# All tiles of a diffusion-transformer block on multiples of 64 bytes, the large ones on multiples of 2048

## The chip, the cores and the metric

The kernel runs on one core of a Trainium2 chip. The metric is the device time of one execution in microseconds; three executions were timed, and a further one was recorded by the hardware profiler. Everything about the profile comes from that one.

A core has a matrix engine (TensorE, PE in the profile, with its weight loads as PEld), VectorE (DVE), ScalarE (ACT), GpSimd (POOL), a queue engine (SP) and 16 DMA engines. Operands lie in an on-chip memory of 128 partitions. A tile has the same byte address in each of its partitions, and that address is what this change is about.

## What is computed

One layer of a diffusion backbone over 256 latent tokens and 256 context tokens of width 2048, in fp32:

```python
mod = jax.nn.silu(c) @ w_mod[layer] + b_mod[layer]
h = modulate(rmsnorm(x, norm_g[layer, 0]), sh_a, sc_a)
hc = modulate(rmsnorm(ctx, norm_g[layer, 0]), csh_a, csc_a)
# one input projection, split: latent attention q/k/v, the recurrent branch, the gates
attn_l = block_attention(q_l, concat(k_c, k_l), concat(v_c, v_l))
hgo_c, s_f, s_b = hgrn2_bidirectional(*hg_c[:6], zero_state, zero_state)
hgo_l, _, _ = hgrn2_bidirectional(*hg_l[:6], s_f, s_b)
out_l = merge_branches(attn_l, hgo_l, hg_l[6], gl_l, ...)     # two branch products, gates, w_out
x = x + gt_a * rmsnorm(out_l, norm_g[layer, 1])
h = modulate(rmsnorm(x, norm_g[layer, 2]), sh_f, sc_f)
x = x + gt_f * rmsnorm(swiglu(h, w_ffn_in[layer], w_ffn_out[layer]), norm_g[layer, 3])
```

The feed-forward width is 44 × 128 = 5632. The weights are read from the chip's main memory once; the profile counts 375 MB of reads.

## The kernel before

**How a product is made.** To keep fp32 accuracy, each operand is split into a high part H and a rest L, and a product is three matmuls: weight H by activation H, weight H by activation L, weight L by activation H. A weight block arrives by DMA as a tile `raw` (128 × 2048, 1 MB, three buffers); `split_w` makes `wH` with a ScalarE copy (L100) and `wL` with a VectorE subtraction (L102), in halves of 1024 columns, three buffers each. Activations are kept split. Tile `hx` (128 × 2 × 16 × 2 × 256: stream, block of the width, H or L, token) holds both streams' activations, and later, unit by unit, the merged branches, the feed-forward input and the feed-forward middle. Eight more units of 512 columns lie in the buffers `hC`. `cqkv` holds the split latents of the attention.

**The forms of a matmul.** One operand is stationary (loaded as weights, 128 columns), the other moves through (256 or 512 columns).

- `mm3` (L136): weights stationary, three matmuls. In `project` with two streams the moving operand is 512 wide, half of it from each stream; with one stream it is 256 wide. The first six blocks go into the sums `pre` while their activations are still being made.
- `mm_wide` (L140, L141): the two products with weight H are one matmul, since H and L of an activation lie side by side in `hx`: 512 columns; then weight L by activation H, 256 columns. The gate blocks (`ps`) and the feed-forward input (`psf`) use it.
- `project_tok` (L816): the activation is stationary and the weights move, 512 wide, into sums `pst` of 128 tokens by 512 channels. The output projection and the feed-forward output use it. A unit of the activation serves as six matmuls: two halves of the tokens, three products. In the last column block of some passes the weights are split into other tiles (`split_into`): into unused units of `hx`, or into `hC` buffers named `wl`.
- L754: the two branch products, 256 wide, moving `hx` (attention) and then `hC` (recurrent branch).

**Order.** The stages follow one another: modulation and first blocks (to about 150 us), the recurrent heads (to 566), gates and attention (to 822), branch products (to 915), output projection (to 1005), norm (to 1044), then feed-forward input and output in three parts each. A scheduler puts the instructions of each engine into one order ahead of time; it works with the sizes of the operations.

**Where the tiles lie.** Pools are laid out one after another in the order of their opening: `cp` (constants and `hx`), `wp` (`raw`, `wH`, `wL`), `ap` (`hC`), `bp` (four-unit tiles and `cqkv`), `wk` (small and middle-sized work tiles). Inside a pool the tiles lie in order of first use, each rounded up to 32 bytes. `cp` starts at byte 16,512, a multiple of 64. Its first tiles are `ones` (512 bytes), `epst` (4, rounded to 32), `sm` (924, to 928), `c0` (520, to 544), `cn` (3584), `cst` (8192), `A1` and `SH1` (128 each). Three of these are an odd number of 32-byte steps, so `hx` comes to byte 30,560, which is 32 past a multiple of 64 and 1888 past a multiple of 2048; `cn`, `cst` and `kr` are 32 past a multiple of 64 too. `wp` starts at 99,072, and from there `raw`, `wH`, `wL`, `hC` and the `bp` tiles all lie 768 past a multiple of 2048, that is, on multiples of 256. The later half of `wk` (from the tile `rdec` on) is again 32 past a multiple of 64.

Of the constants, `ones` is written once by VectorE at L62 and read by the sums of squares (`norm_x` at L212, `latent` at L383, L553); `cn` is loaded by one DMA from ScalarE's queue (L367) and read first by `rope` (L395). `rstd_tok` and `rstd_bcast` are called by nothing.

Of the kernel before, what the change touches and what calls it, by code (L numbers as in the profile page):

```python
# [7 lines left out]
F32 = mybir.dt.float32  # L8
F32R = mybir.dt.float32r
U32 = mybir.dt.uint32  # L10
AF = mybir.ActivationFunctionType
ALU = mybir.AluOpType
PSUM = bass.MemoryType.PSUM

P = 128
T = 256
D = 2048
KD = D // P
NH = 8
# [7 lines left out]
def block_kernel(  # L27
# [21 lines left out]
    nc = tc.nc  # L49

    cp = ctx.enter_context(tc.tile_pool(name="cp", bufs=1))
# [3 lines left out]
    wk = ctx.enter_context(tc.tile_pool(name="wk", bufs=1))  # L55
    pj = ctx.enter_context(tc.tile_pool(name="pj", bufs=4, space=PSUM))
    px = ctx.enter_context(tc.tile_pool(name="px", bufs=4, space=PSUM))
    dp = ctx.enter_context(tc.tile_pool(name="dp", bufs=1, space=bass.MemoryType.DRAM))


    ones = cp.tile([P, P], F32, name="ones")
    nc.vector.memset(ones, 1.0)  # L62
    epst = cp.tile([P, 1], F32, name="epst")
    nc.vector.memset(epst, EPS)

    sm = cp.tile([P, 231], F32, name="sm")
    nc.sync.dma_start(sm, small)
# [6 lines left out]
    ogt = sm[:, 230:231]  # L74
    c0 = cp.tile([P, 130], F32, name="c0")
    nc.scalar.dma_start(c0, consts[:, 0:130])
    ident = c0[:, 0:128]
    sel = c0[:, 128:130]
    cn = cp.tile([P, 896], F32, name="cn")
    perm = cn[:, 0:128]  # L80
# [67 lines left out]

    def rstd_tok(sums, n, tag):

        pt = px.tile([P, 512], F32, tag="px", name="ptok")
        for hf in range(2):
            for i, a in enumerate(sums):
                nc.tensor.matmul(pt[:, hf:hf + 1], a[:, hf * P:(hf + 1) * P], ones[:, 0:1],
                                 start=(hf == 0 and i == 0), stop=(hf == 1 and i == len(sums) - 1))
        return rstd_bcast(pt, n, tag)

    def rstd_bcast(pt, n, tag):
        rt = wk.tile([P, 2], F32, tag="rtok", name="rtok")
        nc.scalar.activation(rt, pt[:, 0:2], AF.Sqrt, bias=epst, scale=1.0 / n)  # L160
        nc.vector.reciprocal(rt, rt)
        dg = wk.tile([P, 2, P], F32, tag="dg", name="dg")
        pb = px.tile([P, 512], F32, tag="px", name="pbc")
        for hf in range(2):
            nc.vector.tensor_scalar(dg[:, hf], ident, rt[:, hf:hf + 1], None, op0=ALU.mult)
            nc.tensor.matmul(pb[:, hf * P:(hf + 1) * P], ones, dg[:, hf], start=(hf == 0), stop=(hf == 1))
        r = wk.tile([P, T], F32, tag=tag, name="rb")
        nc.scalar.copy(r, pb[:, 0:T])
        return r


# [3 lines left out]

    cst = cp.tile([P, D], F32, tag="cst", name="cst")[:, 0:KD * 32].rearrange("p (k m) -> p k m", m=32)
    nc.gpsimd.memset(cst, 0.0)
    nc.vector.tensor_copy(cst[:, :, 0:2], cv)

    A1 = cp.tile([P, KD, 2], F32, name="A1")  # L180
    SH1 = cp.tile([P, KD, 2], F32, name="SH1")

    hx = cp.tile([P, 2, KD, 2, T], F32R, name="hx")

# [91 lines left out]
    for g, nk in enumerate(GROUPS + [0, 0]):  # L278
# [3 lines left out]
        for kt in range(nt):  # L282
            if nk:
                raw = ahead.pop(0) if ahead else load_w(wm1[tile_no])
                tile_no += 1
                n = 256 * nk
                per = 2048 // n
                for kk in range(per):
                    k = kt * per + kk
                    nc.tensor.matmul(pm[32 * (k % 4):32 * (k % 4) + 32, 0:n], cst[:, k], raw[:, kk * n:(kk + 1) * n],  # L290
                                     start=(k < 4), stop=(k >= KD - 4))
# [9 lines left out]
        pt = px.tile([P, 512], F32, tag="px", name="pt")  # L301
# [20 lines left out]
    nc.vector.reciprocal(lbm, lbm)  # L322
    lb = cp.tile([P, 2, NH], F32, name="lb")
    oml = cp.tile([P, 2, NH], F32, name="oml")
    nc.vector.tensor_tensor(lb, lbt[:, 0], lbm, op=ALU.mult)
    nc.vector.tensor_scalar(oml, lb, -1.0, 1.0, op0=ALU.mult, op1=ALU.add)


    mod2 = cp.tile([P, 4, KD], F32, name="mod2")
    cbt = []  # L330
# [35 lines left out]

    nc.scalar.dma_start(cn, consts[:, 130:1026])  # L367

# [20 lines left out]

    kr = cp.tile([P, 2 * T], F32, name="kr")  # L390
    latent([0, 1], (0, 1), 512, kvgt, ckvs, 256, ("f", "kk"))
# [52 lines left out]
    def hgrn_head(h):  # L444
# [11 lines left out]
        def gate_chain(d, psf):  # L456
# [12 lines left out]
            qsv = qs.rearrange("p (n t) -> p n t", n=4)  # L469
            dec = wk.tile([P, 5], F32, tag=f"dec{d}", name=f"dec{d}")  # L470
            rdec = wk.tile([P, 4], F32, tag="rdec", name="rdec")
            fc = f[:, T:2 * T]
# [207 lines left out]
    def att_s(i, A):  # L680
# [4 lines left out]
        for qb in range(2):  # L685
# [5 lines left out]
            for n, (a, b) in enumerate(((0, 0), (0, 1), (1, 0))):  # L691
                nc.tensor.matmul(psS, qr[a][rr, qsl], krs[b][rr, :], start=False, stop=(n == 2))  # L692
            mx = wk.tile([P, 4], F32, tag="mx", name="mx", bufs=2)
            nc.vector.reduce_max(mx[:, 0:1], psS, axis=mybir.AxisListType.X)  # L694
# [73 lines left out]
    b2 = bm.rearrange("p (a k) -> p a k", k=KD)  # L768
    gts = cp.tile([P, 2, KD], F32, name="gts")
    A2 = cp.tile([P, KD], F32, name="A2")  # L770
    SH2 = cp.tile([P, KD], F32, name="SH2")
    nc.vector.tensor_tensor(SH2, mod2[:, 1], b2[:, 3], op=ALU.add)
# [46 lines left out]
    def sqrt_table(dep):  # L819

        t_ = wk.tile([P, 1], F32, tag="rdec", name="tbl")
        nc.scalar.activation(t_, dep, AF.Sqrt)

    def rstd_part(i, hf):

        rt = cp.tile([P, 1], F32, name=f"rt{i}{hf}")
        nc.vector.tensor_reduce(rt, ssq[:, i, hf], axis=mybir.AxisListType.X, op=ALU.add)
        nc.scalar.activation(rt, rt, AF.Sqrt, bias=epst, scale=1.0 / D)
        nc.vector.reciprocal(rt, rt)
        return rt  # L830
# [9 lines left out]
    r1 = []  # L840
    ssq = cp.tile([P, 3, 2, 4], F32, name="ssq")
    for c in range(4):
# [279 lines left out]
```

## Time and profile before

| | us |
|---|---|
| median of 3 timed runs (lowest, highest) | 1770.2 (1769.6, 1770.48) |
| the profiled execution | 1770.05 |
| its span, first to last instruction | 1768.3 |
| mean granted TensorE clock | 0.992 |

The profile gives, for each engine, its busy time and what ended its idle time; it groups instructions by source line, engine, operation and tiles. In `psf<-hx,wH 128*128 128x512` the sum `psf` is made from `hx` and `wH`, with a stationary operand of 128 × 128 and a moving one of 128 × 512. [...] The clock column is the share of the full TensorE clock that was granted.

### The profile page before, as it was taken

How to read it: one execution, taken by the hardware profiler on the slowest of the kernel's cores; microseconds unless marked ns; L12 is line 12 of the kernel's file. 1: busy time of each engine (PE TensorE's matmuls, PEld its weight loads, DVE VectorE, ACT ScalarE, POOL GpSimd, SP SyncE). 2: the span in 40 equal slices, each digit the busy share in tenths (PEclk: the TensorE clock that was granted, in tenths of full speed). 3: DMA queues.
4: the chain of work that ended last, by engine and by line, in shares of the span. 5: the costliest groups of instructions: out<-in, count | busy, mean ns of one | idle time of the engine just before them, and what ended most of it. 6: DMA issues, size and time to landing. Idle time of an engine off the chain costs nothing.

```text
span 1768.3 us, 24307 instructions
## 1 busy us (share of the span) xinstructions
PE 1719.5 (97%) x9696; PEld 1455.7 (82%) x9696; DVE 1114.2 (63%) x1702; ACT 781.7 (44%) x1162; POOL 55.6 (3%) x85
## 2 busy tenths in 40 slices
PE   5898999999999999999999899999999999999997
PEld 3457988888889888889998698888888888888886
DVE  5335777776768766666764687776445555555555
ACT  5224433333334544445544654444444444344443
POOL 1100000000000000001210000000000000000000
PEclk9999999999999999999999899999999999999999
DMA  9884355554556565578765457776555555555553
GB/s 385 324 331 164 122 194 209 191 197 168 194 180 227 208 226 215 191 262 316 277 233 184 163 208 271 289 283 259 190 190 191 189 184 187 191 186 187 188 189 119
DMA packets 59329, 382.87 MB, mean 217 GB/s; under 512 B 7024, under 2 KB 7568, under 8 KB 15952
## 3 DMA queue, kind: packets, MB, share of 16 engines
q1 hardware_dynamic: 54000, 365.85, 57.3%
q0 software_dynamic: 4352, 13.90, 2.1%
q8 instruction: 76, 1.25, 0.3%
q10 hardware_dynamic: 864, 1.57, 0.2%
q14 instruction: 37, 0.30, 0.0%
HBM read 374.99 MB, written 6.31 MB: 216 GB/s over the span
## 4 chain that ended last, share of the span: by engine, by line
PE 96%; DMA 2%; DVE 1%; ACT 1%; issue 0%; DVEq 0%; SPq 0%; ACTq 0%
PE ps L136 20%; PE pst L816 19%; PE psf L140 18%; PE psf L141 9%; PE ps L140 7%; PE psb L754 5%; PE pre L136 4%; PE ps L141 3%; PE psf L915 1%; PE pm L290 1%; DMA raw<-in_wm_dram 1%; PE psS L692 1%; PE po L716 1%; PE psS L689 1%; PE pv L664 1%; PE pq L648 1%
## 5 line engine op out<-in xcount | busy, mean ns | idle before, releaser
L102 DVE TENSOR_TENSOR wL<-raw,wH 128x1024 fp32r<-128x1024 f32 x480 | 588.2, 1227 | 458.4 <-ACT wH L100 456.6
L100 ACT CAST wH<-raw 128x1024 fp32r<-128x1024 f32 x480 | 501.6, 1046 | 745.2 <-PE ps L136 194.7
L140 PE MATMUL psf<-hx,wH 128*128 128x512 f32 x1344 | 470.8, 393 | 0.0
L141 PE MATMUL psf<-hx,wL 128*128 128x256 f32 x1344 | 374.9, 279 | 0.0
L136 PE MATMUL ps<-hx,wH 128*128 128x512 f32 (+1 forms) x1312 | 334.1, 343 | 1.3 <-ACT lat L380 1.3
L140 PEld LDWEIGHTS psf<-hx,wH 128*128 128x128 f32 x1344 | 251.8, 187 | 60.0
L141 PEld LDWEIGHTS psf<-hx,wL 128*128 128x128 f32 x1344 | 251.8, 187 | 0.3
L136 PEld LDWEIGHTS ps<-hx,wH 128*128 128x128 f32 x1312 | 225.0, 188 | 31.3 <-ACT lat L380 1.5
L816 PE MATMUL pst<-wH,hx 128*128 128x512 f32 x800 | 237.2, 396 | 0.0
L136 PE MATMUL ps<-hx,wL 128*128 128x512 f32 (+1 forms) x656 | 225.1, 343 | 1.2 <-DVE wL L102 1.2
L140 PE MATMUL ps<-hx,wH 128*128 128x512 f32 x512 | 184.4, 399 | 0.0
L816 PEld LDWEIGHTS pst<-wH,hx 128*128 128x128 f32 x800 | 150.5, 188 | 36.5
L349 DVE CUSTOM_DVE_ANT_0 raw<-raw,cb 128x2048 f32<-128x2048 f32 x64 | 146.2, 2284 | 42.6 <-DMA raw<-in_wm_dram 41.9
L141 PE MATMUL ps<-hx,wL 128*128 128x256 f32 x512 | 143.7, 281 | 0.0
L816 PE MATMUL pst<-wL,hx 128*128 128x512 f32 x400 | 143.5, 396 | 0.0
L136 PEld LDWEIGHTS ps<-hx,wL 128*128 128x128 f32 x656 | 123.7, 189 | 16.6 <-DVE wL L102 1.4
L140 PEld LDWEIGHTS ps<-hx,wH 128*128 128x128 f32 x512 | 96.0, 188 | 23.2 <-issue 1.7
L141 PEld LDWEIGHTS ps<-hx,wL 128*128 128x128 f32 x512 | 96.2, 188 | 2.4 <-DVE mx L694 1.1
L816 PEld LDWEIGHTS pst<-wL,hx 128*128 128x128 f32 x400 | 75.3, 188 | 18.4
L136 PE MATMUL pre<-hx,wH 128*128 128x512 f32 x192 | 66.0, 424 | 4.6 <-ACT hx L220 4.5
L136 PEld LDWEIGHTS pre<-hx,wH 128*128 128x128 f32 x192 | 37.5, 201 | 26.0 <-ACT hx L220 10.9
L754 PE MATMUL psb<-hx,wH 128*128 128x256 f32 x256 | 46.8, 282 | 0.0
(427 smaller groups left out, 1742.0 us busy)
## 6 DMA issues: line engine op xcount, KB each, us to landing
raw<-in_wm_dram SPq DMA_DIRECT2D x96, 1024.0 KB, 5.2
raw<-in_wfi_dram SPq DMA_DIRECT2D x84, 1024.0 KB, 4.8
raw<-in_win_dram SPq DMA_DIRECT2D x73, 1024.0 KB, 4.8
raw<-in_wfo_dram SPq DMA_DIRECT2D x44, 1024.0 KB, 4.8
raw<-in_wbr_dram SPq DMA_DIRECT2D x16, 1024.0 KB, 5.9
raw<-in_wout_dram SPq DMA_DIRECT2D x16, 1024.0 KB, 4.8
raw<-in_wqk_dram SPq DMA_DIRECT2D x4, 1024.0 KB, 5.3
sgd<-sgx POOLq DMA_DIRECT2D x16, 256.0 KB, 5.5
```

Source lines behind the costliest of these rows:

```text
L100: nc.scalar.copy(H, raw[:, o:o + n])
L102: nc.vector.tensor_tensor(L, raw[:, o:o + n], H.bitcast(F32), op=ALU.subtract)
L136: nc.tensor.matmul(o, l, r, start=(first and i == 0), stop=(last and i == len(seq) - 1))
L140: nc.tensor.matmul(ps, w[0], act.rearrange("p e t -> p (e t)"), start=first, stop=False)
L141: nc.tensor.matmul(ps[:, 0:T], w[1], act[:, 0, :], start=False, stop=last)
L290: nc.tensor.matmul(pm[32 * (k % 4):32 * (k % 4) + 32, 0:n], cst[:, k], raw[:, kk * n:(kk + 1) * n], start=(k < 4), stop=(k >= KD - 4))
L349: nc.vector.tensor_tensor_reduce(out=raw, in0=raw, in1=cbt[0], scale=1.0, scalar=0.0, op0=ALU.mult, op1=ALU.add, accum_out=mod2[:, i // KD ...
L648: nc.tensor.matmul(pq[:, i * T:(i + 1) * T], l, r, start=(k == 0 and i == 0 and z == 0), stop=(k == 3 and i == 1 and z == 2))
L664: nc.tensor.matmul(pv[:, i, :], ckvs[:, k, l, ts_], r, start=(i == 0 and k == 0 and z == 0), stop=(i == 1 and k == 1 and z == 2))
L689: nc.tensor.matmul(psS, qn[a][:, i * T + qb * P:i * T + (qb + 1) * P], kn[b], start=(n == 0), stop=False)
L754: nc.tensor.matmul(ps[:, br * T:(br + 1) * T], l, r, start=(br == 0 and k == 0 and z == 0), stop=(br == 1 and k == NH - 1 and z == 2))
L816: mm = nc.tensor.matmul(ps[hf], l, r, start=(k == 0 and n == 0), stop=(k == nk - 1 and n == 2))
```

## The change

Sizes of tiles are padded, some tiles change their pool or their place in it, and slices keep the part that is used. No instruction of the computation is added or taken away. The diff, cut to its core:

```diff
-    ones = cp.tile([P, P], F32, name="ones")
-    nc.vector.memset(ones, 1.0)
-    epst = cp.tile([P, 1], F32, name="epst")
+    epst = cp.tile([P, 16], F32, name="epst")[:, 0:1]
...
-    sm = cp.tile([P, 231], F32, name="sm")
+    sm = cp.tile([P, 256], F32, name="sm")[:, 0:231]
...
-    c0 = cp.tile([P, 130], F32, name="c0")
+    c0 = cp.tile([P, 144], F32, name="c0")[:, 0:130]
...
-    cn = cp.tile([P, 896], F32, name="cn")
+    A1 = cp.tile([P, KD, 2], F32, name="A1")
+    SH1 = cp.tile([P, KD, 2], F32, name="SH1")
+    kr = cp.tile([P, 2 * T], F32, name="kr")
+    hx = cp.tile([P, 2, KD, 2, T], F32R, name="hx")
+    cst_t = cp.tile([P, D], F32, tag="cst", name="cst")
+    cn = cp.tile([P, 1024], F32, name="cn")
+    ones = cn[:, 896:1024]
+    nc.vector.memset(ones, 1.0)
...
-    def rstd_tok(sums, n, tag):
...
-    def rstd_bcast(pt, n, tag):
...
-    cst = cp.tile([P, D], F32, tag="cst", name="cst")[:, 0:KD * 32].rearrange("p (k m) -> p k m", m=32)
+    cst = cst_t[:, 0:KD * 32].rearrange("p (k m) -> p k m", m=32)
...
-    lb = cp.tile([P, 2, NH], F32, name="lb")
-    oml = cp.tile([P, 2, NH], F32, name="oml")
+    lb = wk.tile([P, 2, NH], F32, name="lb")
+    oml = wk.tile([P, 2, NH], F32, name="oml")
...
-    nc.scalar.dma_start(cn, consts[:, 130:1026])
+    nc.scalar.dma_start(cn[:, 0:896], consts[:, 130:1026])
...
-            dec = wk.tile([P, 5], F32, tag=f"dec{d}", name=f"dec{d}")
-            rdec = wk.tile([P, 4], F32, tag="rdec", name="rdec")
+            dec = wk.tile([P, 16], F32, tag=f"dec{d}", name=f"dec{d}")[:, 0:5]
+            rdec = wk.tile([P, 16], F32, tag="rdec", name="rdec")[:, 0:4]
...
-            mx = wk.tile([P, 4], F32, tag="mx", name="mx", bufs=2)
+            mx = wk.tile([P, 16], F32, tag="mx", name="mx", bufs=2)[:, 0:4]
...
-        rt = cp.tile([P, 1], F32, name=f"rt{i}{hf}")
+        rt = wk.tile([P, 16], F32, name=f"rt{i}{hf}")[:, 0:1]
```

In the same way `mod2`, `gts`, `A2`, `SH2` and `ssq` go from `cp` to `wk`, `ssq` and the small tile of `sqrt_table` padded.

By the sizes, `cp` then holds `epst` (64 bytes), `sm` (1024), `c0` (576), `A1`, `SH1` (128 each), which end at 18,432 = 9 × 2048; `kr` (2048) ends at 20,480, where `hx` begins; `cst` follows at 86,016, `cn` at 94,208, and the pool ends at 98,304 = 48 × 2048. So `hx`, `raw`, `wH`, `wL`, `hC` and the `bp` tiles all begin on multiples of 2048, and each tile of `wk` on a multiple of 64. The distance between two tiles of `wp`, `ap` and `bp` stays what it was; that between any of them and `hx` changes.

More of the change, by code (lines that the diff above doesn't have):

```diff
@@ L147, in rstd_from @@
         return r
-    def rstd_tok(sums, n, tag):
[L151 to L156, printed above, removed]
-    def rstd_bcast(pt, n, tag):
[L159 to L169, printed above, removed]
     sg = wk.tile([P, KD, 2], F32, tag="csig", name="csig")
@@ L174, in block_kernel @@
     nc.vector.tensor_tensor(cv, cv, sg, op=ALU.mult)
-    cst = cp.tile([P, D], F32, tag="cst", name="cst")[:, 0:KD * 32].rearrange("p (k m) -> p k m", m=32)
+    cst = cst_t[:, 0:KD * 32].rearrange("p (k m) -> p k m", m=32)
     nc.gpsimd.memset(cst, 0.0)
     nc.vector.tensor_copy(cst[:, :, 0:2], cv)
-    A1 = cp.tile([P, KD, 2], F32, name="A1")
-    SH1 = cp.tile([P, KD, 2], F32, name="SH1")
-    hx = cp.tile([P, 2, KD, 2, T], F32R, name="hx")
     def both(k, e):
@@ L322, in block_kernel @@
     nc.vector.reciprocal(lbm, lbm)
-    lb = cp.tile([P, 2, NH], F32, name="lb")
-    oml = cp.tile([P, 2, NH], F32, name="oml")
+    lb = wk.tile([P, 2, NH], F32, name="lb")
+    oml = wk.tile([P, 2, NH], F32, name="oml")
     nc.vector.tensor_tensor(lb, lbt[:, 0], lbm, op=ALU.mult)
     nc.vector.tensor_scalar(oml, lb, -1.0, 1.0, op0=ALU.mult, op1=ALU.add)
-    mod2 = cp.tile([P, 4, KD], F32, name="mod2")
+    mod2 = wk.tile([P, 4, KD], F32, name="mod2")
     cbt = []
@@ L388, in latent @@
             split_act(dst[:, i], r)
-    kr = cp.tile([P, 2 * T], F32, name="kr")
     latent([0, 1], (0, 1), 512, kvgt, ckvs, 256, ("f", "kk"))
@@ L768, in block_kernel @@
     b2 = bm.rearrange("p (a k) -> p a k", k=KD)
-    gts = cp.tile([P, 2, KD], F32, name="gts")
-    A2 = cp.tile([P, KD], F32, name="A2")
-    SH2 = cp.tile([P, KD], F32, name="SH2")
+    gts = wk.tile([P, 2, KD], F32, name="gts")
+    A2 = wk.tile([P, KD], F32, name="A2")
+    SH2 = wk.tile([P, KD], F32, name="SH2")
     nc.vector.tensor_tensor(SH2, mod2[:, 1], b2[:, 3], op=ALU.add)
@@ L819, in sqrt_table @@
     def sqrt_table(dep):
-        t_ = wk.tile([P, 1], F32, tag="rdec", name="tbl")
+        t_ = wk.tile([P, 16], F32, tag="rdec", name="tbl")[:, 0:1]
         nc.scalar.activation(t_, dep, AF.Sqrt)
     def rstd_part(i, hf):
-        rt = cp.tile([P, 1], F32, name=f"rt{i}{hf}")
+        rt = wk.tile([P, 16], F32, name=f"rt{i}{hf}")[:, 0:1]
         nc.vector.tensor_reduce(rt, ssq[:, i, hf], axis=mybir.AxisListType.X, op=ALU.add)
@@ L840, in block_kernel @@
     r1 = []
-    ssq = cp.tile([P, 3, 2, 4], F32, name="ssq")
+    ssq = wk.tile([P, 32], F32, name="ssq")[:, 0:24].rearrange("p (i h c) -> p i h c", i=3, h=2)
     for c in range(4):
```

## The prediction

> **What bounds the kernel now.** I read the page's head first, then its chain of waits.
>
> ```profile
> span 1768.3 us, 24307 instructions
> ...
> PE 1719.5 (97%) x9696; PEld 1455.7 (82%) x9696; DVE 1114.2 (63%) x1702; ACT 781.7 (44%) x1162; POOL 55.6 (3%) x85
> ...
> PE 96%; DMA 2%; DVE 1%; ACT 1%; issue 0%; DVEq 0%; SPq 0%; ACTq 0%
> ```
>
> The first line is the span, the second the busy time of each engine, the third the chain that ended last, by engine: 96% of it is TensorE. Next I asked for the busy time in stretches, to see where that is not so.
>
> ```profile
> 0.00:150.00 150.00, 120.55 (x672) 73.20 (x673) 63.09 (x155) 49.53 (x100) 17.70 (x35) 0.97 0.86 334
> ...
> 190.00:566.00 376.00, 376.00 (x2154) 327.21 (x2153) 281.31 (x580) 141.11 (x189) 0.00 (x0) 1.00 0.53 186
> ...
> 1044.00:1220.00 176.00, 176.00 (x1009) 153.43 (x1009) 132.55 (x160) 85.60 (x130) 0.00 (x0) 1.00 0.76 283
> ```
>
> Columns: the stretch, its length, then busy time and count of PE, PEld, DVE, ACT, POOL, then granted clock, DMA share and GB/s. From 190 us on TensorE is busy the whole time at clock 1.00 while VectorE, ScalarE and the DMA engines have room. So a nanosecond taken from a matmul there comes off the span. In the first 150 us the DMA engines are 86% busy and TensorE waits for them in part.
>
> The change moves data without taking work away, so what matters is whether the same matmul takes another time on another address. The groups of instructions, shapes kept apart, show that it does (busy us, then mean ns of one):
>
> ```profile
> L140 PE MATMUL psf<-hx,wH 128*128 128x512 f32 x1344 | 470.8, 393 | 0.0
> ...
> L816 PE MATMUL pst<-wH,hx 128*128 128x512 f32 x800 | 237.2, 396 | 0.0
> L136 PE MATMUL ps<-hx,wH 128*128 128x512 f32 x672 | 215.6, 399 | 0.0
> L140 PE MATMUL ps<-hx,wH 128*128 128x512 f32 x512 | 184.4, 399 | 0.0
> ...
> L816 PE MATMUL pst<-wL,hx 128*128 128x512 f32 x400 | 143.5, 396 | 0.0
> L136 PE MATMUL ps<-hx,wL 128*128 128x512 f32 x336 | 133.6, 398 | 0.0
> ...
> L136 PE MATMUL pre<-hx,wH 128*128 128x512 f32 x192 | 66.0, 424 | 4.6 <-ACT hx L220 4.5
> ...
> L136 PE MATMUL pre<-hx,wL 128*128 128x512 f32 x96 | 39.2, 408 | 0.0
> L816 PE MATMUL pst<-wH,hC 128*128 128x512 f32 x128 | 37.0, 389 | 0.0
> ...
> L816 PE MATMUL pst<-wl,hx 128*128 128x512 f32 x24 | 5.9, 396 | 0.0
> L816 PE MATMUL pst<-hx 128*128 128x512 f32 x24 | 5.8, 390 | 0.0
> ```
>
> The four kinds of L816 do the same product: one operand is the activation (in hx or hC), the other the weight halves (in wH/wL, in hC as "wl", or in hx). hx starts 32 bytes past a multiple of 64; the pools with wH, wL and hC start on multiples of 64. Both operands on multiples of 64: 389 ns. Both in hx, 32 past it: 390. One of each: 396, either way round. These lengths overlap, so I take the distance from start to start out of the timeline (start, length, what, how many in a row):
>
> ```profile
> 1500.43 1.10 PE L816 MATMUL pst<-wH,hx 128*128 128x512 f32 x4
> ...
> 1511.67 1.07 PE L816 MATMUL pst<-wH,hC 128*128 128x512 f32 x4
> ...
> 1522.56 1.10 PE L816 MATMUL pst<-wH,hx 128*128 128x512 f32 x4
> ```
>
> Between the first two lines lie 48 matmuls with the activation in hx (8 units, two halves, three products): 11.24 us, 234.2 ns each. Between the last two lie 48 with it in hC: 10.89 us, 226.9 ns. Same pass, same output, same weight pool: **7.3 ns a matmul**.
>
> **The change part by part.** After it hx, the weight buffers and hC all start on multiples of 2048. *Activation stationary, L816:* 800+400+24 = 1224 matmuls pair hx with a pool. They become the hC case, both operands still at the same distances of 512 bytes from one another: 1224 × 7.3 ns = **8.9 us**. Those with hC and the 24 with hx alone already have one phase: 0. The bound from below is 0, if the place and not the phase made the difference.
>
> *Activation moving, 512 columns then 256 (L140, L141):* 1344+512 = 1856 pairs.
>
> ```profile
> 1600.11 0.39 PE L140 MATMUL psf<-hx,wH 128*128 128x512 f32 x1
> 1600.34 0.28 PE L141 MATMUL psf<-hx,wL 128*128 128x256 f32 x1
> ...
> 1604.31 0.39 PE L140 MATMUL psf<-hx,wH 128*128 128x512 f32 x1
> ```
>
> Twelve pairs in 4.20 us: 350.0 ns a pair. No pair of this form is aligned in this trace. The aligned 512 of L816 takes 226.9; an aligned 256 is seen in L754, whose second half moves hC and whose first half moves hx:
>
> ```profile
> 842.96 0.40 PE L754 MATMUL psb<-hC,wH 128*128 128x256 f32 x2
> ...
> 845.83 0.40 PE L754 MATMUL psb<-hx,wH 128*128 128x256 f32 x2
> ...
> 848.71 0.40 PE L754 MATMUL psb<-hC,wH 128*128 128x256 f32 x2
> ```
>
> 24 matmuls from hC take 2.87 us, 24 from hx 2.88: 119.6 and 120.0 ns. So 256 columns cost the same on either address, and I put all of them at **0** (L136's and L915's too). An aligned pair is then 226.9 + 120.0 = 346.9, and 3.1 ns × 1856 = **5.8 us**. From above: the 256 in the pair stays at some 118 (the rows give 233 + 117), so 5.1 × 1856 = 9.5. From below I use the rows of cqkv, a moving tile on a multiple of 64 against wH, 512 wide:
>
> ```profile
> 655.04 0.62 PE L136 MATMUL pk<-cqkv,wH 128*128 128x512 f32 x2
> 655.50 0.40 PE L136 MATMUL pk<-cqkv,wL 128*128 128x512 f32 x1
> 655.73 0.28 PE L141 MATMUL ps<-hx,wL 128*128 128x256 f32 x1
> ```
>
> Three in 0.69 us, 230 ns. That is not 227, though these three stand alone among misaligned ones. A pair of 230 + 120 gains 0. I take the L816 value, since it is a steady run.
>
> *Activation moving, 512 columns, both streams (L136):* 672+336 = 1008.
>
> ```profile
> 278.53 0.63 PE L136 MATMUL ps<-hx,wH 128*128 128x512 f32 x2
> ...
> 289.03 0.40 PE L136 MATMUL ps<-hx,wH 128*128 128x256 f32 x2
> ```
>
> 45 matmuls in 10.50 us: 233.3 ns. At 226.9 that is 6.4 × 1008 = **6.5 us**; at 230, 3.3 us. The 192+96 of the first stage gain 1.8 us if TensorE bounds them; with the DMA engines at 86% I count half, **0.9** (0 to 1.8).
>
> *The ones in cn, small tiles moved, two unused functions gone:* ones is written at the start as before, only into the tail of cn, whose load must then not be held back. All that touches cn shows (count, shortest, median and longest ns, first and last start):
>
> ```profile
> L395 PE MATMUL pw<-kr,cn x2: 377/378/378, 155.1 to 155.3; 128*128 128x256 f32 x2
> L367 ACTq DMA_DIRECT2D cn<-in_consts_dram x1: 457/457/457, 1.2 to 1.2; - x1
> ```
>
> The load writes columns 0 to 895, ones is 896 to 1023. Were they nevertheless taken for one piece, the load, now issued at 1.2 us, would wait on ScalarE's queue for the two norm_x that read ones. cn's first reader comes at 155.1, so some 150 us hide it. If that cover were gone, 448 KB at the stage's 334 GB/s are 1.3 us, gained or lost. I take 0. Copies, casts and loads keep their sizes, and DVE and ACT have room: 0. What is late next after a faster matmul? Nothing at 190 us and later: VectorE, the busiest other, has 281 of 376 us in its worst long stretch.
>
> [...]
>
> **Sum:** 8.9 + 5.8 + 6.5 + 0.9 = 22.1 us. The profiled execution took 1770.05 us (span 1768.3 and 1.75 around it), 0.15 under the median 1770.2 of the runs. Forecast **1748 us**. All terms at their best, 8.9 + 9.5 + 6.5 + 1.8 = 26.7: 1743. At the low ends of the moving forms, 8.9 + 0 + 3.3 + 0 = 12.2: 1758.
>
> **The rivals.** Both operands in hx, in the timeline:
>
> ```profile
> 996.40 2.91 PE L816 MATMUL pst<-hx 128*128 128x512 f32 x12
> ```
>
> *Only the stationary form gains.* For it: the cqkv rows, at 230. Against it: these 12 take 2.91 us with the last one's whole 0.39 in it, so (2.91 − 0.39) / 11 = 229 ns each, and 390 ns in the groups; it is the relation that counts and not which operand is off. Time 1770 − 8.9 = 1761; if the 256 of each pair rises from 118 to 120 besides, 3.7 back: 1765.
>
> *The place, not the phase.* hx lies low in the partition and hC near the weights; what L816 shows could hang on that, and moving hx by some 10 KB changes nothing. Time 1770. Against it: hx with hx, 390, and "wl" in hC against hx, 396. [...]
>
> *Slower: one phase for everything is the bad one when the activation moves.* With hx and wH both at 0 of 2048, the two reads of each L140 or L136 would start level each time. For it: the third cqkv matmul above is 0.40 us long, and lengths exceed distances by 389 − 227 = 162 ns, so it took 233 to 243 ns, some 236. At 236 + 120 a pair loses 6.0 × 1856 = 11.1, L136 loses 2.7 × 1008 = 2.7, L816 gives 8.9 back: 1775. It decides from 8.9 us / 2864, that is 3.1 ns lost per 512-wide matmul. Against it: L816's steady 226.9 has its operands level as well.
>
> **How the numbers follow.** Forecast, from 1739 to 1757, 0.64; only the stationary form or little more, 1757 to 1766, 0.16; no change 0.12; slower 0.08. The range 1739 to 1765 holds about 0.8: it takes in the best sum with 4 us for attention and small tiles, which I did not count, and the 1765 of the first rival. About 0.2%, 3.5 us, is what a measurement of this kernel can tell from no change. Faster 0.80, within it 0.12, slower 0.08.
>
> **What would show it.** L816 on hx at 389 ns mean in the groups, hC unchanged; pairs of L140 and L141 at 347 ns start to start; L136 at 227; L754 at 120 in both halves; stretches after 190 us still 100% TensorE. Wrong, if L816 on hx stays at 396, if L140 rises, or if idle time of PE behind wL or raw appears where there was none.

## The result, and the profile after

| | before | after |
|---|---|---|
| median of the runs, us | 1770.27 | 1759.39 |
| span of the profiled execution, us | 1768.3 | 1757.2 |
| mean granted TensorE clock | 0.992 | 0.991 |

The ratio is 0.994, with a 95% interval of 0.9928 to 0.9952. The change gains 10.9 us. The forecast was 1748, a gain of 22: the time lies inside the range, but half of the expected gain is missing. The instructions of every engine are the same, and in the same order but for two fills of constants on VectorE at the start, so the traces can be laid side by side; in the new file L136, L140, L141, L754, L816 and L915 are L143, L147, L148, L733, L795 and L894.

The head of the page of after, and its chain of waits by engine:

```profile
span 1757.2 us, 24307 instructions
...
PE 1707.3 (97%) x9696; PEld 1456.5 (83%) x9696; DVE 1112.8 (63%) x1702; ACT 780.9 (44%) x1162; POOL 59.0 (3%) x85
...
PE 95%; DMA 2%; ACT 1%; DVE 1%; issue 0%; SPq 0%; DVEq 0%; ACTq 0%
```

TensorE still bounds it. The span fell by 11.1 us and TensorE's busy time by 12.2, the other engines' hardly. So the time went out of the matmuls; TensorE idles some 1 us longer, in the first stage, and no other wait took anything back. The groups of instructions of after, shapes apart (busy us, mean ns of one):

```profile
L147 PE MATMUL psf<-hx,wH 128*128 128x512 f32 x1344 | 475.2, 399 | 0.0
...
L795 PE MATMUL pst<-wH,hx 128*128 128x512 f32 x800 | 231.3, 389 | 0.0
L143 PE MATMUL ps<-hx,wH 128*128 128x512 f32 x672 | 212.3, 394 | 0.0
...
L143 PE MATMUL pre<-hx,wH 128*128 128x512 f32 x192 | 66.7, 430 | 6.0 <-ACT hx L200 5.9
```

The stationary form fell from 396 to 389 and the form with both streams from 399 to 394, as forecast. But the 512-wide half of the feed-forward pairs rose from 393 to 399. Lengths overlap (the stationary form of after is 389 ns long at starts 226.8 apart), so the pace has to be read from starts. The chain gives it for whole stages; of before it shows (start, length, what, pieces):

```profile
1220.50 89.97 PE pst L816 x384
1489.67 88.54 PE pst L816 x384
```

And of after:

```profile
1213.11 87.08 PE pst L795 x384
1481.08 87.10 PE pst L795 x384
```

The first output pass, 384 stationary matmuls, went from 89.97 to 87.08 us. Between it and the second lie the 512 pairs of the second part of the feed-forward input: 1489.67 − (1220.50 + 89.97) = 179.20 us before, 350.0 ns a pair, and 1481.08 − (1213.11 + 87.08) = 180.89 after, **353.3**. The pairs became slower. The timeline of after shows how:

```profile
1403.90 0.40 PE L147 MATMUL psf<-hx,wH 128*128 128x512 f32 x1
1404.13 0.28 PE L148 MATMUL psf<-hx,wL 128*128 128x256 f32 x1
1404.25 0.40 PE L147 MATMUL psf<-hx,wH 128*128 128x512 f32 x1
1404.48 0.28 PE L148 MATMUL psf<-hx,wL 128*128 128x256 f32 x1
1404.60 0.40 PE L147 MATMUL psf<-hx,wH 128*128 128x512 f32 x1
1404.84 0.28 PE L148 MATMUL psf<-hx,wL 128*128 128x256 f32 x1
1404.96 0.40 PE L147 MATMUL psf<-hx,wH 128*128 128x512 f32 x1
```

From one 512 to the next: 0.35, 0.35, 0.36 us. In the trace's nanoseconds the pairs run 236 + 113, 233 + 117, 241 + 120, and again from the start, for whole stages. Before, each pair of this stage was 231 + 118 or 233 + 118.

The form with both streams in the timeline of after, a first row of 512 columns and the first of 256 behind it:

```profile
277.20 0.62 PE L143 MATMUL ps<-hx,wH 128*128 128x512 f32 x2
...
286.73 0.40 PE L143 MATMUL ps<-hx,wH 128*128 128x256 f32 x2
```

42 matmuls lie between them, 9.53 us: 226.9 ns each, down from 233.3.

All distances from the start of one matmul to the start of the next, after minus before, added up by the form of the first of the two:

| form | forecast, us | measured, us |
|---|---|---|
| stationary, L816 | −8.9 | −9.2 |
| both streams, 512 wide, L136 | −6.5 | −5.3 |
| pairs, L140 and L141 | −5.8 | +3.9 (feed-forward +4.4, gates −0.5) |
| 256 wide (L136, L754, L915) | 0 | +0.3 |
| first stage (`pre`) | −0.9 | +0.1 |
| sum | −22.1 | −10.2 |

The span's other 0.9 us are in none of these forms. The stages ahead of the first output pass vary by more than that by themselves: a second profile of the changed kernel reached the first output pass at 1217.15 instead of 1213.11 us and from there on was the same.

### The profile page after: what moved, and what is told of

Same layout as the page of the kernel before. It is cut to its first block, busy times and chain, and to the rows that moved or that the text cites. A ratio compares the mean times of both kernels' runs of the same rounds, so it can differ in the third digit from the quotient of the medians.

```text
span 1757.2 us, 24307 instructions
## 1 busy us (share of the span) xinstructions
PE 1707.3 (97%) x9696; PEld 1456.5 (83%) x9696; DVE 1112.8 (63%) x1702; ACT 780.9 (44%) x1162; POOL 59.0 (3%) x85
## 4 chain that ended last, share of the span: by engine, by line
PE 95%; DMA 2%; ACT 1%; DVE 1%; issue 0%; SPq 0%; DVEq 0%; ACTq 0%
PE ps L143 20%; PE pst L795 18%; PE psf L147 18%; PE psf L148 9%; PE ps L147 7%; PE psb L733 5%; PE pre L143 4%; PE ps L148 3%; PE psf L894 1%; DMA raw<-in_wm_dram 1%; PE pm L270 1%; PE psS L671 1%; PE po L695 1%; PE psS L668 1%; PE pv L643 1%; PE pq L627 1%
## 5 line engine op out<-in xcount | busy, mean ns | idle before, releaser
L147 PE MATMUL psf<-hx,wH 128*128 128x512 f32 x1344 | 475.2, 399 | 0.0
L148 PE MATMUL psf<-hx,wL 128*128 128x256 f32 x1344 | 377.4, 281 | 0.0
L143 PE MATMUL ps<-hx,wH 128*128 128x512 f32 (+1 forms) x1312 | 330.6, 341 | 1.3 <-ACT lat L360 1.3
L147 PEld LDWEIGHTS psf<-hx,wH 128*128 128x128 f32 x1344 | 252.6, 188 | 62.6
L148 PEld LDWEIGHTS psf<-hx,wL 128*128 128x128 f32 x1344 | 253.9, 189 | 0.3
L143 PEld LDWEIGHTS ps<-hx,wH 128*128 128x128 f32 x1312 | 226.1, 190 | 28.4 <-ACT lat L360 1.5
L795 PE MATMUL pst<-wH,hx 128*128 128x512 f32 x800 | 231.3, 389 | 0.0
L143 PE MATMUL ps<-hx,wL 128*128 128x512 f32 (+1 forms) x656 | 223.8, 341 | 1.2 <-DVE wL L109 1.2
L147 PE MATMUL ps<-hx,wH 128*128 128x512 f32 x512 | 184.0, 400 | 0.0
L795 PEld LDWEIGHTS pst<-wH,hx 128*128 128x128 f32 x800 | 150.0, 188 | 31.2
L148 PE MATMUL ps<-hx,wL 128*128 128x256 f32 x512 | 143.6, 281 | 0.0
L795 PE MATMUL pst<-wL,hx 128*128 128x512 f32 x400 | 140.6, 389 | 0.0
L143 PEld LDWEIGHTS ps<-hx,wL 128*128 128x128 f32 x656 | 124.4, 190 | 14.4 <-DVE wL L109 1.4
L147 PEld LDWEIGHTS ps<-hx,wH 128*128 128x128 f32 x512 | 96.1, 188 | 23.0 <-issue 1.7
L148 PEld LDWEIGHTS ps<-hx,wL 128*128 128x128 f32 x512 | 96.5, 189 | 2.4 <-DVE mx L673 1.1
L795 PEld LDWEIGHTS pst<-wL,hx 128*128 128x128 f32 x400 | 75.1, 188 | 15.6
L143 PE MATMUL pre<-hx,wH 128*128 128x512 f32 x192 | 66.7, 430 | 6.0 <-ACT hx L200 5.9
L143 PEld LDWEIGHTS pre<-hx,wH 128*128 128x128 f32 x192 | 38.4, 206 | 26.6 <-ACT hx L200 13.6
L733 PE MATMUL psb<-hx,wH 128*128 128x256 f32 x256 | 46.8, 283 | 0.0
```

What stands on the lines that cost most here:

```text
L143: nc.tensor.matmul(o, l, r, start=(first and i == 0), stop=(last and i == len(seq) - 1))
L147: nc.tensor.matmul(ps, w[0], act.rearrange("p e t -> p (e t)"), start=first, stop=False)
L148: nc.tensor.matmul(ps[:, 0:T], w[1], act[:, 0, :], start=False, stop=last)
L733: nc.tensor.matmul(ps[:, br * T:(br + 1) * T], l, r, start=(br == 0 and k == 0 and z == 0), stop=(br == 1 and k == NH - 1 and z == 2))
L795: mm = nc.tensor.matmul(ps[hf], l, r, start=(k == 0 and n == 0), stop=(k == nk - 1 and n == 2))
```

## The experiments

The expectations number their theories. Theory 1: what counts is the distance between the two tiles of a matmul within 64 bytes. Theory 2: the cost needs the other engines or the transfers. Theory 3: the distance counts, but in other steps than 64, finer or coarser; later it is the distance modulo 256. Theories 4 and 5 ask whether a stream's pace is set by what ran before it or by where all its tiles lie together, and theory 6 asks the latter of the kernel. The standing rival is that round addresses carry the gain: multiples of 64 or 2048, or the small tiles that moved. By the addresses given above, the weights lay at 0 modulo 256 before and after, and `hx` went from 96 to 0.

Five kernels, whose labels begin with m, leave the layer out: they run bare streams of matmuls with the kernel's shapes, one after another, and write a few of the sums. Beside them ScalarE copies eight columns after each stream (in the runs of entries and of shifts also one small tile, as a pause), and once the operands are loaded no other engine works. The mean granted clock was 0.998 to 1.0. Their cases are functions of byte offsets, `r` of the activation, `h` and `l` of the two weight halves:

```python
def pair(r, h=0, l=0):   # as mm_wide; still, dual, narrow: as L816, L136 with two streams and with one
    ...
    a = (k % 8) * 1024 + r // 4
    ops.append((512, wa[:, h // 4 + k * P:h // 4 + k * P + P], act[:, a:a + 512]))
    ops.append((256, wb[:, l // 4 + k * P:l // 4 + k * P + P], act[:, a:a + 256]))
```

### Offsets, in streams alone

```python
for n, r in zip(lt, (0, 16, 32, 48, 64, 96, 128, 256, 512, 1024)): res.append(("pair" + n, pair(r)))
for n, r in zip(lt, (0, 16, 32, 48, 64, 128)): res.append(("still" + n, still(r)))   # dual alike
...
```

> This kernel leaves out the whole layer and runs only streams of matmuls of the four forms on tiles at chosen byte offsets, with nothing else on the chip's engines; its time says nothing about the layer. Theory 1, the cost is set by how far the two operands of a matmul lie from one another within 64 bytes: activation stationary and 512 columns moving, 227 ns apart at distance 0, 234 at 32; both streams (512 in two pieces), 227 and 233; pairs of 512 and 256, 353.3 ns at distance 0 in a cycle of three pairs, 350.0 at 32; 256 alone 120 at each; distances of 64, 128, 256, 512, 1024 like 0. Theory 2, the cost needs the other engines or the transfers: all distances give the same. Theory 3, finer or coarser steps count: 16 and 48, or 64 and 512, differ from 0 and 32 in their own way.

Groups of this run:

```profile
L78 PE MATMUL stillc<-wa,act 128*128 128x512 f32 x64 | 20.1, 395 | 0.0
...
L78 PE MATMUL dualc<-act,wa 128*128 128x512 f32 x64 | 20.1, 395 | 0.0
...
L78 PE MATMUL stilla<-wa,act 128*128 128x512 f32 x64 | 19.7, 389 | 0.0
...
L78 PE MATMUL duala<-act,wa 128*128 128x512 f32 x64 | 19.7, 389 | 0.0
L78 PE MATMUL paira<-act,wa 128*128 128x512 f32 x48 | 17.3, 403 | 0.0
...
L78 PE MATMUL pairf<-act,wa 128*128 128x512 f32 x48 | 16.8, 393 | 0.0
```

`a` is distance 0, `c` 32, `f` 96. Offset 0 gives 389, as the stationary form has it after the change, and 32 gives 395, close to its 396 before, here in the two-stream form as well, while the pairs are at their longest at 0; at 96, the distance of the kernel before, they have its 393. Start to start, pairs settle at 353.3 ns at 0, 346.7 at 16 and at 32, 350.0 at 96, 351.1 at 128, and 353.3 again at 256, 512 and 1024. So both the gain and the loss come with the address, the DMA engines and VectorE idle, which ends theory 2, and the pairs repeat at 256 bytes. At 64, a multiple of 64, the stationary form is at 233.3: that multiple isn't what it asks for, and theory 1 with its step of 64 falls.

### The change with `hx` 32 bytes back

```diff
-    sm = cp.tile([P, 256], F32, name="sm")[:, 0:231]
+    sm = cp.tile([P, 248], F32, name="sm")[:, 0:231]
...
     hx = cp.tile([P, 2, KD, 2, T], F32R, name="hx")
+    hpad = cp.tile([P, 8], F32, name="hpad")
+    nc.vector.memset(hpad, 0.0)
```

> The changed kernel with hx (and c0, A1, SH1, kr before it) 32 bytes lower, everything else left on the multiples of 2048. Theory 1 (distance of hx to the weight tiles within 64 bytes is all): the result of before comes back, 1770 us (1767 to 1772), with L795 at 396 ns, both-stream L143 at 399 and pairs of L147 and L148 at 350.0 ns start to start. Rival (the multiples of 2048, ones in cn, the small tiles in wk carry the gain): stays at 1759 us.

1765.93 us, ratio 0.9979 (0.997 to 0.9989). Its groups:

```profile
L149 PE MATMUL psf<-hx,wH 128*128 128x512 f32 x1344 | 469.8, 394 | 0.0
...
L797 PE MATMUL pst<-wH,hx 128*128 128x512 f32 x800 | 236.4, 395 | 0.0
L145 PE MATMUL ps<-hx,wH 128*128 128x512 f32 x672 | 215.5, 399 | 0.0
```

Stationary and two-stream forms are back where they were before the change. It isn't 1770: `hx` lies at 224 modulo 256 now, not at 96. Laid beside the trace of before, no form explains that alone: the matmuls of 256 columns in L136 gain 1.3 us, the first stage 1.2, the stationary form 1.1, the branch products 0.7, the pairs 0.5. The pairs are not those of before even so. Its chain:

```profile
1214.83 89.60 PE pst L797 x384
1485.32 88.34 PE pst L797 x384
1684.60 67.21 PE pst L797 x288
```

The 512 pairs after the first pass take 1485.32 − 1304.43 = 180.89 us, 353.3 each; the 320 after the second take 1684.60 − 1573.66 = 110.94, 346.7 each. The same loop, at the same distance, has two paces in two stages. No theory expected that.

### The kernel before with `hx` on a multiple of 64 only

```diff
-    epst = cp.tile([P, 1], F32, name="epst")
+    epst = cp.tile([P, 16], F32, name="epst")[:, 0:1]
...
-    ssq = cp.tile([P, 3, 2, 4], F32, name="ssq")
+    ssq = cp.tile([P, 32], F32, name="ssq")[:, 0:24].rearrange("p (i h c) -> p i h c", i=3, h=2)
```

> The kernel before with two tiles padded (epst to 64 bytes, ssq to 128), so that hx comes to a multiple of 64 and the pools behind it stay on multiples of 64, none on 2048; hx lies 64 bytes off the weight tiles within 512. Theory 1: all of the change's 10.9 us, 1759 us, pairs at 353.3 ns. Theory 3 (within 512): the stationary form at 227 but pairs at another value than 353.3, time 1748 to 1757 or 1761 to 1768. Rival (2048 needed): 1770 us.

1761.86 us, ratio 0.9954 (0.9937 to 0.9971). This alone could be read as "64 is enough". The group that the prediction's largest term stands on says otherwise:

```profile
L816 PE MATMUL pst<-wH,hx 128*128 128x512 f32 x800 | 236.5, 395 | 0.0
L136 PE MATMUL ps<-hx,wH 128*128 128x512 f32 x672 | 213.1, 396 | 0.0
```

Now 64 from the weights within 256 bytes, the stationary form keeps its slow pace and gains 1.1 us in all; what came was some 4 us of the two-stream form, some 2 of the 256-wide one, and 2.5 in the first stage, which varies by as much. The feed-forward pairs run at 353.3 in the first part and 348.9 in the other two. A like time, made of other terms.

### The whole map

```python
for f, fn in (("pair", pair), ("still", still), ("dual", dual), ("narrow", narrow)):
    for n in range(16): res.append((f + "R" + lt[n], fn(16 * n)))
    for n in range(1, 16): res.append((f + "L" + lt[n], fn(0, 0, 16 * n)))
    res.append((f + "Sc", fn(32, 32, 32))); res.append((f + "Sg", fn(96, 96, 96)))
```

> Again streams of matmuls alone, the layer left out: the four forms at every distance of 16 bytes from 0 to 240 between the activation and the weights (R), at every such offset of the low weight half alone (L), and with all operands moved together by 32 or 96 bytes (S). Theory 3 (the distance modulo 256 bytes sets a fixed rhythm): S gives the values of distance 0 (pairs 353.2, stationary and both-stream 226.7, 256 wide 120.0); distance 96 gives the values of the kernel before (pairs 350.0, stationary 233 to 234, both-stream 233); the L cases leave pairs at 346.7 for most offsets. Rival (absolute place): S differs from distance 0.

Ns from start to start, by the distance of the activation from the weights in bytes:

| | 0 | 16 | 32 | 64 | 96 | 128 | 192 | 224 | 240 |
|---|---|---|---|---|---|---|---|---|---|
| stationary | 226.7 | 226.7 | 233.3 | 233.3 | 234.3 | 233.3 | 228.9 | 233.3 | 226.7 |
| two streams | 226.7 | 231.7 | 233.3 | 228.9 | 233.3 | 232.4 | 233.3 | 233.3 | 226.7 |
| pairs | 353.3 | 346.7 | 346.7 | 353.3 | 350.0 | 351.1 | 353.3 | 346.7 | 353.3 |
| 256 wide | 120.0 | 118.7 | 116.7 | 117.8 | 120.0 | 118.7 | 113.3 | 118.3 | 117.2 |

Each is the settled pace of one stream behind one other, and not every one is the only pace of its distance: at 64 the pairs had taken 348.9 in the run of offsets. No distance is best for all. At 0 the first two forms have their best and the pairs their worst. One expectation failed: with everything shifted by 32 or 96 together, which leaves the distance at 0, the stationary and two-stream forms kept 226.7, but the pairs took 346.7 and not 353.2. With weight L alone moved by 48 to 80 bytes the pairs take 346.7, and weight H can stay. That points to a version better than both: everything at 0, and only the L half of the pairs' weights 64 bytes off.

### How a stream is entered

```python
entries = (("D", dual(0)[:18]), ("N", narrow(0)[:18]), ("T", still(0)[:18]), ("P", pair(48)[:18]), ("G", None))
for name, ops in (("z", pair(0)), ("lx", pair(0, 0, 64)), ("s", pair(32, 32, 32)), ...):
    for e, first in entries: res += [("e" + e, first), (name + "X" + e, ops)]
```

> Streams of matmuls alone, the layer left out; each form started behind five different streams (both-stream, 256 wide, stationary, pairs at distance 48, and a pause). Theory 4, pairs at distance 0 have two steady rhythms and fall into one by how they are entered: for them some of the five starts give 346.7 ns and some 353.3. Theory 5, the absolute place decides (a shift of all operands by 32 bytes gave 346.7): all five starts at distance 0 give 353.3 and all five with the shift 346.7. The low weight half 48, 64 or 80 bytes later, or all weights 32 bytes lower (activation at 32): 346.7 from each start if that rhythm is the only one there; stationary and both-stream form at 0: 226.7 from each start.

Pairs at distance 0, first and last of 32 in the timeline, behind 256-wide matmuls (`zXN`) and behind pairs at another distance (`zXP`), and with L moved by 64 (`lxXD`):

```profile
82.83 0.40 PE L78 MATMUL zXN<-act,wa 128*128 128x512 f32 x1
...
93.78 0.40 PE L78 MATMUL zXN<-act,wa 128*128 128x512 f32 x1
...
112.67 0.40 PE L78 MATMUL zXP<-act,wa 128*128 128x512 f32 x1
...
123.42 0.39 PE L78 MATMUL zXP<-act,wa 128*128 128x512 f32 x1
...
140.35 0.39 PE L78 MATMUL lxXD<-act,wa 128*128 128x512 f32 x1
...
151.10 0.39 PE L78 MATMUL lxXD<-act,wa 128*128 128x512 f32 x1
```

31 distances in 10.95, 10.75 and 10.75 us: 353.2, 346.8 and 346.8 ns. The same instructions on the same addresses have two steady paces, and which of them comes goes with what ran before. So the prediction's 346.9 exists at distance 0; of five entries one finds it, and the kernel's don't. With L 64 off all five entries give 346.7. The stationary and two-stream forms at 0 came to 226.7 behind every entry, within some eight matmuls. Grouping two 512s and two 256s gave 348.3 a pair, four and four 350.8. One case speaks against the distance as the whole of it: with both weight halves 32 up and the activation left, a distance of 224, the pairs took 353.3 behind all five entries, where the map, with the activation at 224, had 346.7.

### Only the distance modulo 256

```diff
+    hpad = cp.tile([P, 40], F32, name="hpad")
+    nc.vector.memset(hpad, 0.0)
     hx = cp.tile([P, 2, KD, 2, T], F32R, name="hx")
+    hpad2 = cp.tile([P, 24], F32, name="hpad2")
+    nc.vector.memset(hpad2, 0.0)
```

The kernel before, with 160 bytes ahead of `hx` and 96 behind it: distance 0 modulo 256, but 1024 modulo 2048, no tile padded, `ones` and the small tiles where they were.

> The kernel before with 160 bytes in front of hx and 96 behind it, nothing else: hx and the weight pools then lie a multiple of 256 apart (1024 within 2048). Theory 3 (the distance within 256 bytes is what the change altered): the whole result of the change, 1759 us (0.993 to 0.995 of before), with the stationary form at 389 ns, both-stream at 227 start to start and pairs at 353.3. Rival (2048, the small tiles or ones in cn have a part): between 1761 and 1770.

1758.7 us, ratio 0.9945 (0.9932 to 0.9957): the whole effect of the change. Its groups are those of after:

```profile
L140 PE MATMUL psf<-hx,wH 128*128 128x512 f32 x1344 | 475.2, 399 | 0.0
...
L820 PE MATMUL pst<-wH,hx 128*128 128x512 f32 x800 | 231.3, 389 | 0.0
L136 PE MATMUL ps<-hx,wH 128*128 128x512 f32 x672 | 212.3, 394 | 0.0
```

Added up by form, its distances differ from those of before by the same −9.2 us (stationary), −5.3 (two streams), +4.4 and −0.5 (pairs) as the change. The common 2048, the small tiles, their change of pool and `ones` inside `cn` have no part in it that these runs could show.

### The change, and weight L of the pairs 64 bytes further

```diff
-            L = pool.tile([P, n], F32R, tag=tags[1], name="wL", bufs=bufs)
+            L = pool.tile([P, n + (64 if pool is wp else 0)], F32R, tag=tags[1], name="wL", bufs=bufs)[:, lo:lo + n]
...
-            w = split_w(load_w(wfi[2 * (j - 2) + i]))
+            w = split_w(load_w(wfi[2 * (j - 2) + i]), lo=16)
```

The same `lo=16` stands in the gate blocks. To make room, `epst` goes into the unused end of `sm`'s tile and the small `rt` tiles become one; by the sizes, all large tiles then lie 64 bytes lower together.

> The changed kernel, in which the low weight half of the pairs (gate blocks and feed-forward input) lies 64 bytes later in a tile 256 bytes longer; the six small rt tiles are one and epst lies behind sm to make room. Theory 3: pairs go from 353.3 to 346.7 ns start to start, 6.6 ns x 1856 = 12 us, and nothing else moves: 1747 us, 0.987 of before. Rival (in the full kernel ACT, DVE and the transfers set the rhythm of the pairs): 1757 to 1761.

**1747.73 us**, ratio 0.9875 (0.9861 to 0.989), against 1760.34 and 0.9945 (0.9931 to 0.9959) for the change itself, run again beside it:

> The changed kernel as it is, for a comparison on the same chip: 0.994 of before; all theories.

Groups of the version with L moved, and its chain:

```profile
L148 PE MATMUL psf<-hx,wH 128*128 128x512 f32 x1344 | 466.4, 392 | 0.0
...
L796 PE MATMUL pst<-wH,hx 128*128 128x512 f32 x800 | 231.2, 389 | 0.0
```

```profile
1207.33 87.09 PE pst L796 x384
1471.91 87.09 PE pst L796 x384
```

1471.91 − 1294.42 = 177.49 us for 512 pairs, 346.7 each, and the stationary form keeps its 389. 6.6 ns on 1344 feed-forward pairs are 8.9 us, and the 512 gate pairs fell by some 2 ns each, 1.1 us: 10.0 of the 12.6. The rest is the first stage, which varies by as much, and the scatter of the medians. No run of the kernel moved all tiles by 64 and left L where it was, so the two are not quite parted; in streams, with L moved and nothing else, all five entries gave 346.7.

### Shifts of everything together

```python
forms = [("pairS" + lt[n], pair(16 * n, 16 * n, 16 * n)) for n in (0, 1, 2, 3, 4, 6, 8, 12)]
forms += [("narrowR" + lt[n], narrow(16 * n)) for n in (2, 7, 12)]
...
```

> Streams alone, the layer left out. Pairs with all operands moved together by 0, 16, 32, 48, 64, 96, 128, 192 bytes, five starts each: if the absolute place within 256 bytes has a part, some shifts give 346.7 from every start while 0 gives 353 from four of five; if only the start decides, each shift shows both values. 256 wide with the activation at 32, 112 and 192, five starts: 116.7, 113.3 and 113.3 if these are the only steady rhythms. 256 wide with the low weight half alone moved by 16 to 240: near 118, at 144 near 115.6.

In the run of entries, pairs with all operands shifted by 32 had taken 346.7 behind every entry, which spoke for the place of the tiles besides their distance. Here, with the streams in another order, both paces came back at shifts of 32, 64, 96 and 192 (at 32: 346.7 four times, 353.3 once); at 128 it was 353.3 five times. The one answer of the earlier run was not a rule. But shifts that are no multiple of 32 gave a third pace: at 48 all five streams settled at 348.3, at 16 two of them, the other three at 346.7. First and last of 32 pairs at 48:

```profile
309.27 0.40 PE L78 MATMUL pairSdXT<-act,wa 128*128 128x512 f32 x1
...
320.07 0.40 PE L78 MATMUL pairSdXT<-act,wa 128*128 128x512 f32 x1
```

So for the pairs the place of all tiles together counts too, in steps of 16 bytes; the kernel's large tiles all lie on multiples of 32. 256-wide matmuls at distance 112 took 113.3 behind all five entries; at 192, which has 113.3 in the map, two of the five took 117.8, and at 32 two took 117.8 instead of 116.7.

```diff
+    front = cp.tile([P, 8], F32, name="front")
+    nc.vector.memset(front, 0.0)
     epst = cp.tile([P, 16], F32, name="epst")[:, 0:1]
```

The same question in the kernel: one tile of 32 bytes ahead of all others puts every large tile 32 past its multiple and leaves the distances.

> The changed kernel with one 32-byte tile in front of everything: every large tile then begins 32 bytes past a multiple of 64, and all distances between them stay what the change made them. Theory 3 alone (only distances count) and theory 4 (how the pairs are entered): as the changed kernel, 1759 us, pairs at 353.3. Theory 6 (the place of all operands within 256 bytes has a part): pairs at 346.7 as in the streams alone, 1747 us; the other forms stay at 226.7. If multiples of 64 were worth something by themselves: slower than 1759, towards 1770.

1759.91 us, ratio 0.9943 (0.993 to 0.9957), the time of the change, and its groups:

```profile
L149 PE MATMUL psf<-hx,wH 128*128 128x512 f32 x1344 | 475.2, 399 | 0.0
...
L797 PE MATMUL pst<-wH,hx 128*128 128x512 f32 x800 | 231.3, 389 | 0.0
```

The rival of round addresses falls here: no large tile lies on a multiple of 64 any more, and nothing is lost. Theory 6 falls for a shift of 32: the pairs keep 353.3.

### The 256-wide matmuls at their own distance: a miss

```diff
-        w = split_w(load_w(wbr[j]))
+        w = split_w(load_w(wbr[j]), lo=36, hi=36)
```

On top of the version with L moved, both weight halves of the 256-wide blocks go 144 bytes up, so that `hx` is 112 from them modulo 256, where the streams had 113.3 instead of 120.

> The kernel with the low half of the pairs 64 bytes later, and besides both weight halves of the blocks that move 256 columns (one-stream projections, branch products, the last three of the four first feed-forward blocks) 144 bytes later, so that the activation lies 112 bytes behind them within 256; the tile t2 shares the buffers of hf for room. If the distance sets the pace of those too, as in the streams alone: 113.3 instead of 120.0 ns, 6.7 x (960 + 768 + 144) = 12.5 us, 1735 us, 0.981 of before. Rival (these stages are paced by VectorE or by waits once TensorE is faster): 1738 to 1748, with idle time of PE behind wL, wH or DVE results.

1746.83 us, ratio 0.9872 (0.9856 to 0.9889): no gain over 1747.73 beyond the scatter. The branch products stayed at 284 ns in the groups, 119 and 121 in turn from start to start. A last run looked for the reason in streams alone. `ahead` moves the activation up by 112; `behind` moves both weight halves up by 144, which is the same distance modulo 256; in `lowfar` and `highfar` one half lies 256 further. Eight places in steps of 32, two entries each:

```python
forms.append(("ahead" + lt[n], narrow(112 + s, s, s)))
forms.append(("behind" + lt[n], narrow(s, 144 + s, 144 + s)))
forms.append(("lowfar" + lt[n], narrow(s, 144 + s, 400 + s)))
forms.append(("highfar" + lt[n], narrow(s, 400 + s, 144 + s)))
```

> Streams of 256-wide matmuls alone, the layer left out, always with the distance at which 113.3 was measured: the activation 112 bytes ahead of the weights, or 144 behind them (the same within 256, as the kernel had it), or with one weight half 256 bytes further; each at eight places of all operands, two starts. If distances within 256 bytes decide, all give 113.3. If the place of all operands or steps of 512 have a part, as the kernel's unchanged 120.0 suggests, some give 113.3 and others 118 to 120. If all give 113.3, the kernel's 120.0 comes from what the streams alone lack (the other engines, the transfers).

Groups at one of the places (`e`, s = 64):

```profile
L78 PE MATMUL behindeXN<-act,wa 128*128 128x256 f32 x64 | 11.6, 282 | 0.0
L78 PE MATMUL lowfareXN<-act,wa 128*128 128x256 f32 x64 | 11.6, 282 | 0.0
L78 PE MATMUL highfareXN<-act,wa 128*128 128x256 f32 x64 | 11.6, 282 | 0.0
...
L78 PE MATMUL aheadeXN<-act,wa 128*128 128x256 f32 x64 | 11.0, 275 | 0.0
```

All 16 streams of `ahead` ran at 113.3 ns, and all 48 of the others between 116.7 and 120.0, those with a half 256 further exactly as `behind`. So the miss needs no wait to explain it: the kernel's form is `behind`, and `behind` is slow in a bare stream too. In `ahead` the activation lies 16 past a multiple of 32 and the weights on one; in `behind` it is the other way round. For 256-wide matmuls the distance modulo 256 is therefore not all. Moving the activation by 112 in the kernel, which would move all its other forms too, was not tried.

## Why the prediction missed half of the gain

- **That place alone changes the pace of a matmul, and that this bounds the kernel:** right. Bare streams repeat the kernel's 389 and come within 1 ns of its 396, and 256 bytes of padding around `hx` give the whole result. TensorE was not busy the whole time from 190 us on, though: before the change it was busy for 32.94 of the 39 us from 1005 to 1044, at a granted clock of 0.87, and for 67.68 of the last 78.30. One step was wrong: the prediction took a multiple of 64 for both operands as enough, and at a distance of 64 the stationary form stays at 233.3. It cost nothing only because the change took the distance to 0 modulo 256.
- **Stationary form, 7.3 ns × 1224 = 8.9 us:** right in size, 9.2 came, and, but for that step, in mechanism. It rested on two steady runs of the same form inside the trace of before.
- **Two streams, 6.5 us:** right, 5.3 came. The steady pace is the 226.9 ns that the term used. Where a stretch begins or other matmuls come between, several pass before that pace is reached (235, 229, 232 ns and the like at the head of the streams), which the term did not take off. In the bare streams the same form settled at 226.7 to 233.3 ns, by the distance of its tiles.
- **The step that failed is the pair term**, "An aligned pair is then 226.9 + 120.0 = 346.9, and 3.1 ns × 1856 = 5.8 us". It took the paces of two forms, each from a run of its own kind, and added them for a stream in which they alternate. The runs showed that 512 and 256 in turn form a rhythm of their own. At distance 0 it has two steady paces, 346.7 and 353.3; the kernel falls into the second in all three parts of the feed-forward, and the term came out as +3.9 us instead of −5.8. These 9.7 us are most of the 11.2 that are missing. The term's bounds, 0 to 9.5 us gained, left out a loss, although no row showed a pair of this kind at that distance; the text said so itself. The prediction's own sign of being wrong, that L140 rises, is what came: 393 to 399.
- **The rival "only the stationary form gains"** had the band from 1757 to 1766, in which 1759.39 lies. That is a coincidence: the two-stream form gained too, and the pairs took most of that back.
- **The slower rival** ("one phase for everything is the bad one when the activation moves") was right for the feed-forward pairs, with +3.3 ns instead of its 6, and wrong for the two-stream form, where the cqkv matmul it stood on was one at the head of a run, before the pace had settled.
- **Place, not phase:** wrong: moving `hx` by 160 bytes and the weights by 256 gave the whole result, and shifting everything by 32 in the kernel changed nothing.
- **256-wide, `ones` in `cn`, small tiles at 0:** right. The 256-wide form could have gained up to 6.7 ns at other distances (113.3 in a stream), but not at 0. **First stage, 0.9:** not seen; `pre` was busy 0.5 us less in all (its two groups: 66.0 and 39.2 before, 66.7 and 38.0 after), the idle time ahead of the first group 1.4 us longer.
- With the L half moved by 64 bytes, the pair term arrives at 346.7 and the time at 1747.73, beside a forecast of 1748. That is the size of the missing term, not a proof of the prediction, and the agreement is in part luck: laid beside the trace of before, that run gains 9.2 us in the stationary form, 5.2 in the two streams, 6.0 in the pairs, and 2.3 in the first stage, which varies by as much.

What stays open: why these rhythms exist (nothing in the profile shows what a matmul waits for inside TensorE), which entry leads to which pace, how far the place of all tiles together counts beside their distance, and the rule of the 256-wide form.

## What to carry to other kernels

Where matmuls run back to back with new weights each time, lay out the moving and the stationary tiles by their distance, form by form (in the map 226.7 ns at 0 and 233.3 at 64 for the stationary form, 353.3 at 0 and 346.7 at 32 for the pairs), and measure that in a bare stream with the kernel's own sequence of widths and its own placement, behind several entries; round addresses by themselves were worth nothing here (1759.91 us with every large tile 32 bytes off, 1759.39 with none). Don't add the paces of two forms measured apart to price a stream in which they alternate: 226.9 + 120.0 was forecast here, and 353.3 came. Where one layout serves one form and hurts another, an offset on the operand that only the second form uses (here 64 bytes on the L half, some 10 us in the pairs) can have both.

## What the runs showed of the hardware that was not expected

- The pace of a 512-wide fp32 matmul with new weights each time went with the distance of its tiles, 226.7 to 234.3 ns at the distances of the table of the map, with the DMA engines and VectorE idle; in the kernel the stationary form had its 389 ns and the two-stream form its 394 at a distance of 1024 as well as at 0 modulo 2048.
- A stream of alternating widths settled into a fixed cycle (236 + 113, 233 + 117, 241 + 120 ns), and the same stream at the same distance settled into another: 353.3 in one part of the feed-forward and 346.7 in the next (the kernel with `hx` 32 bytes back); 353.3 or 346.7 by what ran before (streams). With all tiles shifted by 48 bytes it was 348.3.
- At one distance modulo 256, 256-wide matmuls took 113.3 ns when the activation lay 16 past a multiple of 32 and the weights on one, and 116.7 to 120.0 the other way round.
